# A row maximum over 64 MB: blocks of 2, 14, 96 and 16 rows per partition in place of 112 and 16

## The chip, the core and the metric

The kernel runs on one core of a Trainium2 chip. Its engines are PE (the matrix engine, whose weight loads are listed as PEld), DVE (the vector engine), ACT (the scalar engine), POOL (the general engine) and SP, which here only issues transfers. Sixteen DMA engines move data between HBM and the on-chip memory, which has 128 partitions. The metric is the time of one execution on the device in microseconds (us). The profile is of one such execution.

## The reference

```python
def setup_inputs():
    batch, seq, dim = 32, 512, 1024
    return {"x": np.random.randn(batch, seq, dim).astype(np.float32)}

def reference(x):
    return np.max(x, axis=-1).astype(np.float32)
```

The input is 16384 rows of 1024 float32 values, 64 MB; the output is the largest value of each row, 64 KB.

## The kernel before

**Blocks.** The 16384 rows are 128 rows for each of the 128 partitions. `BLOCKS` (L13) says how they are dealt out. A block of S rows per partition is a stretch of 128 x S rows that lies in one piece in HBM; partition p holds rows p x S to p x S + S - 1 of it. Before the change there are two blocks, of 112 and of 16 rows per partition (the second list sums to 14, and `last`, 2, comes to it for the tail). Within a block each number of the list is one load: so many rows of every partition, that is 128 runs, one in each partition, each in one piece in HBM. The runs of one load lie S rows (S x 4 KB) apart: 448 KB in the first block, 64 KB in the second. Loads are numbered through all blocks, 0 to 17. Load 0 has 2 rows, load 1 has 15, load 2 has 16.

**The ring.** All loads land in one tile, `ring`, with places for `RING = 47` rows per partition, and go around it: a load that doesn't fit in what is left starts again at place 0. `issue` (the inner function that calls `nc.sync.dma_start`, L238) issues loads in order on SP, each as early in the program as the reductions that read its places have been written down. A load into places that an earlier load had waits on SP until that load's reduction is done, and the loads behind it in SP's queue wait with it. Each load uses one of eight semaphores in turn, and waits too until the load that used it eight loads earlier has landed.

**The order of the work.** `PLAN` (L31) is an order written out by hand. `d3` reduces load 3 on DVE: one instruction for all its rows, written by `maximum` (L78). `t` and `b` steps send parts of some late rows the other way: PE transposes them (L160), ACT copies the result (L166), POOL takes the maximum across partitions (L168), and PE turns the answer back (L178). `p` steps reduce the rest of those rows on DVE, `m` steps merge, and `f0` to `f3` reduce the four pieces into which the last two rows of each partition are cut (loaded at L243). `in_turn` keeps each engine to the order of the plan.

**The stores.** The results lie in the first 128 columns of the ring's tile (`res`), one column for each row of a partition. `views` has one entry for each block: where its results go in HBM, and their columns. All but the last are stored (L265) behind `behind`, which is the reduction `f0`; the last block's store (L267) comes after the last reduction. Both are issued from ACT, after its copies.

What the change touches: `BLOCKS`, and through it the HBM address of every load ahead of load 11, the sizes of loads 1 and 4, the places of loads 2 to 10 in the ring with the reductions that they wait for, and the number of entries in `views`.

Of the kernel before, what the change touches and what calls it, by code (L numbers as in the profile page):

```python
# [10 lines left out]


BLOCKS = [  # L13
    [2, 15, 16, 14, 11, 11, 10, 10, 8, 8, 7],
    [3, 3, 3, 2, 1, 1, 1],
]
RING = 47
# [279 lines left out]
```

## Time and profile before

| | |
|---|---|
| Median of 3 runs | 163.83 us (163.79 to 163.84) |
| Profiled execution, from first to last instruction (span) | 162.1 us |
| DVE busy | 135.3 us (83% of the span), 33 instructions |
| PE, PEld, ACT, POOL busy | 13.6, 11.7, 6.3 and 15.9 us |
| Read from HBM, written | 67.11 MB, 0.07 MB |
| Mean rate over the span | 414 GB/s |

The span is counted within the profiled execution; the median is of whole executions, which hold something more around it. "Idle before" is the time in which an engine had nothing running just before an instruction, and the name behind it is what ended that time. A queue's share is the time that its packets took, out of the time of all 16 DMA engines. A line of the chain of waits that names DMA covers the time from a transfer's issue to its landing, so time spent queued behind other transfers is in it. L numbers are lines of the kernel as printed above.

The reductions, one instruction for each of the loads: 10 rows take 10.82 us (mean of two), 11 rows 11.88, 16 rows 17.22. SP's queue waited 90.8 us in all for reductions (7 times) and 31.2 us for landings of loads (3 times) before it issued at L238. The two stores landed 1.6 and 1.4 us after their issue.

### The profile page before, as it was taken

How to read it: one execution, taken by the hardware profiler on the slowest of the kernel's cores; microseconds unless marked ns; L12 is line 12 of the kernel's file. 1: busy time of each engine (PE TensorE's matmuls, PEld its weight loads, DVE VectorE, ACT ScalarE, POOL GpSimd, SP SyncE). 2: the span in 40 equal slices, each digit the busy share in tenths (PEclk: the TensorE clock that was granted, in tenths of full speed). 3: DMA queues.
4: the chain of work that ended last, by engine and by line, in shares of the span. 5: the costliest groups of instructions: out<-in, count | busy, mean ns of one | idle time of the engine just before them, and what ended most of it. 6: DMA issues, size and time to landing. Idle time of an engine off the chain costs nothing.

```text
span 162.1 us, 295 instructions
## 1 busy us (share of the span) xinstructions
PE 13.6 (8%) x76; PEld 11.7 (7%) x76; DVE 135.3 (83%) x33; ACT 6.3 (4%) x7; POOL 15.9 (10%) x10
## 2 busy tenths in 40 slices
PE   0000000000000000000000000000000000772942
PEld 0000000000000000000000000000000000762731
DVE  3500019998399999999999999996999999999994
ACT  3000000000000000000000000000000000241120
POOL 0000000000000000000000000000000000099791
PEclk9999999999999999999999999999999999996555
DMA  5995999599879999898999799799999989999991
GB/s 178 566 485 258 470 501 517 259 517 517 354 340 439 453 404 534 356 523 367 478 411 475 334 485 475 334 485 388 477 429 388 466 382 446 415 421 416 411 388 34
DMA packets 3456, 67.18 MB, mean 414 GB/s; under 512 B 640, under 2 KB 896, under 8 KB 1536
## 3 DMA queue, kind: packets, MB, share of 16 engines
q1 hardware_dynamic: 3168, 67.11, 96.8%
q10 hardware_dynamic: 288, 0.07, 0.2%
HBM read 67.11 MB, written 0.07 MB: 414 GB/s over the span
## 4 chain that ended last, share of the span: by engine, by line
DMA 50%; DVE 47%; SPq 1%; issue 0%; DVEq 0%
DMA ring<-in_x_dram 50%; DVE ring L78 45%; DVE joint L78 2%; SPq L238 1%; DVEq L292 0%
## 5 line engine op out<-in xcount | busy, mean ns | idle before, releaser
L78 DVE TENSOR_REDUCE ring<-ring 128x1 f32<-128x1024 f32 (+13 forms) x20 | 129.9, 6547 | 23.5 <-DMA ring<-in_x_dram 23.5
L168 POOL PARTITION_ALL_REDUCE top<-sb x6 | 15.7, 2658 | 142.6 <-ACT sb L166 142.5
L160 PE MATMUL ps<-ident,ring 128*128 128x128 f32 x38 | 9.0, 423 | 140.0 <-DMA ring<-in_x_dram 140.0
L160 PEld LDWEIGHTS ps<-ident,ring 128*128 128x128 f32 x38 | 7.6, 225 | 140.1 <-issue 140.1
L166 ACT COPY sb<-ps 128x1024 f32<-128x1024 f32 (+2 forms) x6 | 5.0, 834 | 150.5 <-PE ps L160 143.5
L78 DVE TENSOR_REDUCE joint<-ring 128x2 f32<-128x1280 f32 (+1 forms) x3 | 3.9, 1314 | 0.0
L178 PE MATMUL got<-ident,top 1*128 1x1 f32 x24 | 2.7, 228 | 3.8 <-POOL top L168 3.6
L178 PEld LDWEIGHTS got<-ident,top 1*128 1x128 f32 x24 | 2.4, 188 | 4.6 <-POOL top L168 4.6
L178 PE MATMUL joint<-ident,top 1*128 1x1 f32 x14 | 2.0, 244 | 1.9 <-POOL top L168 1.9
L178 PEld LDWEIGHTS joint<-ident,top 1*128 1x128 f32 x14 | 1.7, 210 | 2.7 <-POOL top L168 2.7
L166 ACT ACT_TABLE_LOAD x1 | 1.3, 1283 | 0.7 <-PEq L281 0.7
L83 DVE MEMSET ident<- 128x128 f32 x1 | 0.2, 165 | 0.8 <-PEq L281 0.8
L90 DVE TENSOR_SCALAR rowno<-rowno 32x1 f32<-32x1 f32 x3 | 0.4, 146 | 0.1
L85 DVE TENSOR_TENSOR_SCAN colno<-ident 128x128 f32<-128x128 f32 x1 | 0.4, 425 | 0.0
L92 DVE TENSOR_SCALAR ident<-colno,rowno 128x128 f32<-128x128 f32 x1 | 0.3, 288 | 0.0
L87 DVE STREAM_TRANSPOSE rowno<-colno 128x32 f32<-128x32 f32 x1 | 0.2, 211 | 0.0
L78 DVE TENSOR_REDUCE ring<-got 128x3 f32<-128x24 f32 x1 | 0.2, 172 | 0.0
L78 DVE TENSOR_REDUCE ring<-joint 128x5 f32<-128x20 f32 x1 | 0.2, 170 | 0.0
L281 POOL MEMSET const-float32-0.0<- 128x1 f32 x1 | 0.1, 98 | 0.2 <-issue 0.2
L281 POOL MEMSET const-bfloat16-1.0<- 128x1 bf16 x1 | 0.1, 102 | 0.0
L281 POOL MEMSET const-uint8-127<- 128x1 uint8 x1 | 0.1, 101 | 0.0
L281 POOL MEMSET const-float32-1.0<- 128x1 f32 x1 | 0.1, 98 | 0.0
(1 smaller groups left out, 0.1 us busy)
## 6 DMA issues: line engine op xcount, KB each, us to landing
ring<-in_x_dram SPq DMA_DIRECT2D x2, 5632.0 KB, 29.9
ring<-in_x_dram SPq DMA_DIRECT2D x2, 5120.0 KB, 36.8
ring<-in_x_dram SPq DMA_DIRECT2D x2, 4096.0 KB, 32.5
ring<-in_x_dram SPq DMA_DIRECT2D x1, 7680.0 KB, 22.6
ring<-in_x_dram SPq DMA_DIRECT2D x1, 7168.0 KB, 58.0
ring<-in_x_dram SPq DMA_DIRECT2D x3, 1536.0 KB, 35.7
ring<-in_x_dram SPq DMA_DIRECT2D x1, 3584.0 KB, 29.2
ring<-in_x_dram SPq DMA_DIRECT2D x2, 1024.0 KB, 17.8
```

Of the source, the lines that this page charges most:

```text
L78: return in_turn("DVE", nc.vector.reduce_max(out=out, in_=in_, axis=X))
L83: in_turn("DVE", nc.vector.memset(ident, 1.0))
L85: in_turn("DVE", nc.vector.tensor_tensor_scan(out=colno, data0=ident, data1=ident, initial=-1.0, op0=ALU.add, op1=ALU.mult))
L87: in_turn("DVE", nc.vector.transpose(out=rowno, in_=colno[:, :32]))
L90: in_turn("DVE", nc.vector.tensor_scalar(out=part, in0=part, scalar1=float(q * 32), scalar2=None, op0=ALU.add))
L92: identity = in_turn("DVE", nc.vector.tensor_scalar(out=ident, in0=colno, scalar1=rowno[:, 0:1], scalar2=None, op0=ALU.is_equal))
L160: in_turn("PE", nc.tensor.transpose(out=ps[:, w:w + P], in_=rows(j)[:, lead[j] + r + i, c * P:(c + 1) * P], identity=ident,))
L166: in_turn("ACT", nc.scalar.copy(out=sb[:, :W], in_=ps[:, :W]))
L168: in_turn("POOL", nc.gpsimd.partition_all_reduce(top[:, :W], sb[:, :W], P, bass_isa.ReduceOp.max))
L178: in_turn("PE", nc.tensor.transpose(out=share(j)[:, r + i, c:c + 1], in_=tops[k][0:1, w:w + P], identity=ident[0:1, 0:1],))
L238: load = nc.sync.dma_start(out=rows(issued), in_=src)
L281: nc = _bacc.Bacc("TRN2", target_bir_lowering=False, num_devices=1)
```

## The change

One list is replaced. The first block's 112 rows per partition become three blocks of 2, 14 and 96.

```diff
 BLOCKS = [
-    [2, 15, 16, 14, 11, 11, 10, 10, 8, 8, 7],
+    [2],
+    [14],
+    [16, 14, 12, 11, 10, 10, 8, 8, 7],
     [3, 3, 3, 2, 1, 1, 1],
 ]
 RING = 47
```

Load 0 is now a whole block of 2 rows per partition, so that its 128 runs of 8 KB lie one behind the other in HBM: one megabyte in one piece. Load 1 is a whole block of 14 rows per partition, seven megabytes in one piece. Loads 2 to 10 read a block of 96 rows per partition, in which the runs of one load lie 384 KB apart. Loads 11 to 17 and the pieces of the tail are as before. Load 1 has 14 rows and not 15, load 4 has 12 and not 11; the number of loads, their order and the plan stay.

There are four entries in `views` and so four stores: three on ACT behind `f0`, of 2, 14 and 96 columns (8, 56 and 384 bytes in each partition), and the last, of 16 columns, as before. The second and third of them wait on semaphores that loads 15 and 16 used.

With 14 rows in load 1, loads 0 to 3 take 46 places, and the loads that go around the ring after them lie elsewhere: load 4 in places 0 to 12 (before: 0 to 11), load 5 in 12 to 23 (11 to 22), load 6 in 23 to 33 (22 to 32), load 7 in 33 to 43 (32 to 42), and loads 8, 9, 10 and on where they were. Load 6 now waits for the reduction of load 3, where before it was load 2's, and load 10 for that of load 5, where before it was load 6's.

## The prediction

> **What bounds the kernel now.** I read the chain of waits first, then the timeline of DVE, the page's DMA queues, and the DMA view cut into short windows. The chain (start, duration, what):
>
> ```profile
> 1.62 41.49 DMA ring<-in_x_dram
> 43.11 0.02 issue
> 43.13 66.55 DVE ring L78 x5
> ...
> 111.01 38.94 DMA ring<-in_x_dram
> ```
>
> Read alone it says DMA, then DVE, then DMA. The timeline of DVE (start, busy time, group, idle time before it and what ended that) shows who really hands over:
>
> ```profile
> 5.65 2.29 DVE L78 TENSOR_REDUCE ring<-ring 128x2 f32<-128x2048 f32 x1 [3.14 <-DMA ring<-in_x_dram]
> 23.78 16.15 DVE L78 TENSOR_REDUCE ring<-ring 128x15 f32<-128x15360 f32 x1 [15.85 <-DMA ring<-in_x_dram]
> 43.13 66.53 DVE L78 TENSOR_REDUCE ring<-ring 128x16 f32<-128x16384 f32 x5 [3.20 <-DMA ring<-in_x_dram]
> 110.97 40.23 DVE L78 TENSOR_REDUCE ring<-ring 128x10 f32<-128x10240 f32 x7 [1.30 <-DMA ring<-in_x_dram]
> ```
>
> DVE waits for a load four times, the last time for load 7 at 110.97. From there it runs with gaps of at most 0.09 us until its last reduction ends at 159.83, 48.9 us. So the end is "landing of load 7, plus 48.9 us of DVE work". Load 7 lands when the load queue has moved the 89 rows per partition of loads 0 to 7, and that queue is never idle (page; packets, MB, share of 16 engines):
>
> ```profile
> q1 hardware_dynamic: 3168, 67.11, 96.8%
> q10 hardware_dynamic: 288, 0.07, 0.2%
> ```
>
> 0.968 x 162.1 = 156.9 us of transfer: all the time from 1.7 us, when the first packets start, to about 158.6. Hence the end moves with the speed of the load stream, and a DVE operation before load 7 can move by up to 1.30 us for nothing.
>
> **The rows moved from load 1 to load 4.** Load 1 goes from 15 rows to 14, load 4 from 11 to 12. Line by form (op, shapes, count, busy us, mean ns):
>
> ```profile
> L78 DVE TENSOR_REDUCE ring<-ring 128x15 f32<-128x15360 f32 x1 | 16.2, 16154 | 15.8 <-DMA ring<-in_x_dram 15.8
> ...
> L78 DVE TENSOR_REDUCE ring<-ring 128x14 f32<-128x14336 f32 x1 | 15.1, 15076 | 0.0
> ```
>
> One row is 16.154 - 15.076 = 1.08 us on DVE. In the stream it is 128 x 4 KB = 0.524 MB, and from 60 to 75 us the stream moved 433 GB/s: 1.21 us. Loads 1, 2 and 3 land 1.21 us earlier; loads 4 onward land when they did, since 58 rows lie up to load 4 in both. DVE: d2 starts at 43.13 - 1.21 = 41.92; the five operations d2 to d6 take 66.53 + 1.08 = 67.61 and end at 109.53 instead of 109.66. DVE then waits 1.4 us for load 7 instead of 1.30. Effect on the end: 0. If the 1.30 us of cover were gone, that 0.13 us would be all it is worth.
>
> **The ring moves.** Loads 0 to 3 now fill 46 of 47 places. Load 4 takes places 0 to 12, load 5 12 to 23, load 6 23 to 33, load 7 33 to 43, load 8 0 to 8, load 9 8 to 16, load 10 16 to 23; from load 11 on places are the old ones. So load 6 now overlaps load 3 and must wait for d3, not d2. On SP it moves from 60.4 to d3's end, about 74.1, and is issued beside load 7, which waited for d3 already: nothing is queued between them that goes later. At 74.1 the stream still has load 5 to move: load 2 (33 rows) was in by 43.13, load 5 ends 36 rows later, 43.13 + 36 x 1.21 = 86.7 us. With 1.0 us from an issue to its first packet (0.72 to 1.7 at the start) the cover is 11 us; below zero, each us would be a us at the end. Load 10 goes the other way, from d6 (109.69) to d5 (98.7); loads 11 to 13, behind it on SP, still wait for d6 and go out at 109.6, with loads 8 and 9 and now 10 ahead of them. Cost 0.
>
> **Two more stores on ACT.** One store of 112 columns becomes three of 2, 14 and 96. All three stand behind the first reduction of the tail pieces and ahead of the last store:
>
> ```profile
> 158.01 0.38 ACTq L265 DMA_DIRECT2D out_dram<-ring  x1
> ...
> 159.66 0.17 DVE L78 TENSOR_REDUCE ring<-joint 128x5 f32<-128x20 f32 x1
> 159.86 0.34 ACTq L267 DMA_DIRECT2D out_dram<-ring  x1
> ```
>
> ACT sits idle from 158.39 to 159.86, waiting for the last reduction. Three issues of 0.38 with 0.05 us between (the gap between SP's issues in the chain) end at 158.01 + 1.24 = 159.25: 0.6 us spare. With SP's dearest issue, 0.61 us, they end at 159.94, and the last store is 0.08 us late. Their packets: q10's 288 took 0.002 x 16 x 162.1 = 5.2 engine-us, 18 ns each. Two stores more are 288 more packets, 0.32 us on each engine, between 159.2 and the last store's packets at 160.7; the loads are over at 158.6. The semaphore waits of the added stores are for loads 15 and 16, whose reductions are over by 156.4. At the end SP has two more completions to look at, at 0.05 us an issue gap 0.1 us. I take 0, the ends are 0 and +0.2.
>
> The Trainium skill (DMA: Bandwidth & Descriptors, Specifications) says that a transfer under 512 B turns into a read-modify-write, which speaks against cutting 448 B runs into 8, 56 and 384 B. Both old stores, 448 B and 64 B, are under that figure already and the row has 18 ns for each packet; by the rule, even at twice that price, the packets would still end before the last store's start.
>
> **The addresses.** Load 0 stays 128 runs of 8 KB, load 1 128 runs of 56 KB; only where the runs begin changes: a pitch of 448 KB becomes 8 KB, 56 KB, and 384 KB for the 96-row block. No row shows those pitches, but the last block is read at 64 KB. The DMA view for a window with 8 KB packets at pitch 448 KB (load 0, 3.2 to 4.4 us) and one with 8 KB packets at pitch 64 KB (load 14, 149.6 to 151.2 us):
>
> ```profile
> q1 hardware_dynamic: 63, 0.52, 101.7%
> ```
>
> ```profile
> q1 hardware_dynamic: 83, 0.68, 101.7%
> ```
>
> 1.017 x 16 x 1.2 / 63 = 0.310 us a packet, and 1.017 x 16 x 1.6 / 83 = 0.314. A seven times smaller pitch, a power of two, moves the price by 1.2%, and windows this short count their edges roughly. I take 0 for the new pitches; the ends are -1.2% and +1.2% of the 109 us up to load 7, -1.3 to +1.3 us. The lower end I trust less: a packet's price is the same all through the big loads, as for an engine at its own limit, so a kinder address should have nothing to give.
>
> The Trainium skill (the same page, Latency and other measured facts) lists 207 GB/s at a row pitch of 512 KiB against 214 with the pitch padded, and advises contiguous tiles or padding: a rule that favours the first two blocks and leaves the third, 3 x 128 KiB, open. By its 3.4% on the whole 96-row block the sum would be some 4 us higher, about 168; 448 and 64 KiB, the pitches of this trace, show nothing of the kind.
>
> The start is the other unknown. The window from 1.6 to 2.6 us, with the rate by its 40 slices (a packet counts where it starts):
>
> ```profile
> GB/s 0 0 0 0 0 983 328 328 0 0 655 328 0 0 0 0 0 328 0 328 328 0 328 328 0 0 0 0 0 0 328 0 328 0 0 0 328 0 0 0
> ...
> q1 hardware_dynamic: 16, 0.13, 77.0%
> ```
>
> 0.770 x 16 x 1.0 / 16 = 0.77 us a packet, 0.46 more than at 3.2 us: the first packets start cold. If scattered addresses cause that, one contiguous megabyte saves up to 0.46 us; if sixteen neighbours get in each other's way, it may cost as much again. I take 0: the sixteen starts are spread over 0.8 of that microsecond, load 0 lands with the engine that starts last, and a late start is set by the issue, which the change leaves as it is.
>
> **Sum.** Span 162.1 + 0 (rows) + 0 (ring) + 0 (stores) + 0 (addresses) = 162.1. Around it lie 163.83 - 162.1 = 1.7 us in the runs shown, which nothing here touches: 163.8.
>
> **Rivals.** (1) The cold start goes away: 163.83 - 0.46 = 163.4. For it, the 0.77 us against 0.31; against it, the engine that starts last. (2) DVE's earlier start reaches the end: 163.83 - 1.21 = 162.6. Against it stands the 1.30 us wait at 110.97, which swallows it. (3) Slower: the 384 KB pitch makes the stream from load 2 on dearer. Each per cent is 0.69 us (the 69 us from 42 to 111), all of it at the end, since DVE waits for load 7 already; it decides from 0.5%, and at 1.2% gives 163.83 + 0.83 = 164.7. For it, the 0.314 against 0.310; against it, the even price of packets at 448 KB. (4) The stores come late by 0.2 to 0.5 us, on ACT or behind 8 B packets: 164.2. Against it, the 0.6 us spare.
>
> **How the numbers follow.** About 0.2% (0.33 us) is what a measurement of this kernel can tell from no change. Forecast, nothing moves by that much: 0.53. Rival 1: 0.15, rival 2: 0.04, together faster 0.19. Rival 3: 0.19, rival 4: 0.09, together slower 0.28. The forecast's own range is 163.5 to 164.15. For 8 in 10 the range goes down to rival 1 and up to most of rival 3: 163.35 to 164.7.
>
> **What would show it.** Right: DVE again waits about 1.4 us for load 7 and starts on it at 111.0 within 0.2; load queue at 96 to 97%; the first packets again near 0.77 us; three store issues done before 159.5 and the last at 159.9. A load 7 landing near 110.5 means rival 1, near 112 rival 3; an ACT issue of the last store long after the last reduction means rival 4. The forecast is wrong most simply if packets of the 96-row block take longer than their size did before.

## The result and the profile after

| | before | changed |
|---|---|---|
| Median | 163.84 us (163.79 to 163.93) | 165.96 us (165.75 to 166.33) |
| Ratio, 95% interval | | 1.013 (1.0118 to 1.0141) |
| Span of the profiled execution | 162.1 us | 163.9 us |

The change costs 2.1 us. The views of the profile show where they are. (The profiled execution of the changed kernel took 165.75 us, the fastest of its runs; its span is 163.95 us with two decimals.) First DVE's timeline, from the first reduction of 16 rows on:

```profile
41.86 67.74 DVE L80 TENSOR_REDUCE ring<-ring 128x16 f32<-128x16384 f32 x5 [4.27 <-DMA ring<-in_x_dram]
110.91 40.23 DVE L80 TENSOR_REDUCE ring<-ring 128x10 f32<-128x10240 f32 x7 [1.30 <-DMA ring<-in_x_dram]
```

Load 2 is there 1.27 us earlier than before (1.21 was forecast), and load 7 starts to be reduced at 110.91, which was 110.97. So nothing was lost in the loads, the ring or the reductions. The timeline of ACT and DVE at the end agrees (start, duration, line):

```profile
157.95 1.34 ACTq L267 DMA_DIRECT2D out_dram<-ring  x3
...
159.61 0.17 DVE L80 TENSOR_REDUCE ring<-joint 128x5 f32<-128x20 f32 x1
159.81 0.34 ACTq L269 DMA_DIRECT2D out_dram<-ring  x1
```

The three stores are issued by 159.29, and the last one leaves at 159.81, 0.05 us earlier than before. The whole loss lies behind that: from the last store's issue to the end of the span it was 162.1 - 159.86 = 2.2 us, and now is 163.95 - 159.81 = 4.1. The page's issues of the stores, in KB and median us from issue to landing, before the change and after it:

```profile
out_dram<-ring ACTq DMA_DIRECT2D x1, 56.0 KB, 1.6
...
out_dram<-ring ACTq DMA_DIRECT2D x1, 8.0 KB, 1.4
```

```profile
out_dram<-ring ACTq DMA_DIRECT2D x1, 48.0 KB, 4.0
...
out_dram<-ring ACTq DMA_DIRECT2D x1, 1.0 KB, 3.0
out_dram<-ring ACTq DMA_DIRECT2D x1, 7.0 KB, 2.7
out_dram<-ring ACTq DMA_DIRECT2D x1, 8.0 KB, 3.2
```

The 8 KB store at the end is the same store in both, and lands 3.2 us after its issue where it took 1.4. SP waits for the landings at the end. Its waits for stores (us in total, times, longest) come to 2.2 us before the change and 4.5 after it:

```profile
SPq L292 <- DMA out_dram<-ring: 2.2, 2, 1.6
```

```profile
SPq L294 <- DMA out_dram<-ring: 4.5, 1, 4.5
```

Yet the packets take no longer. DMA's busy share from 157 to 164 us in 40 slices of 0.175 us, and the queue of the stores in that window (packets, MB, share of 16 engines), before the change and after it:

```profile
DMA  9999998300082000000004000000000000000000
...
q10 hardware_dynamic: 288, 0.07, 4.3%
```

```profile
DMA  9999998300210400730004000000000000000000
...
q10 hardware_dynamic: 576, 0.07, 6.5%
```

0.043 x 16 x 7 us / 288 is 17 ns a packet before the change, and 0.065 x 16 x 7 us / 576 is 13 ns after it. After the loads come four groups in the changed kernel, one for each store; the last is over by 160.9. The packets have gone out, and for two microseconds nothing is busy; only the landings fail to come (the last at 159.81 + 3.2 = 163.0). A packet's time, then, doesn't say when a store has landed.

### The profile page after: what moved, and what is told of

Same layout as the page of the kernel before. It is cut to its first block, busy times and chain, and to the rows that moved or that the text cites. A ratio compares the mean times of both kernels' runs of the same rounds, so it can differ in the third digit from the quotient of the medians.

```text
span 163.9 us, 296 instructions
## 1 busy us (share of the span) xinstructions
PE 12.8 (8%) x76; PEld 11.0 (7%) x76; DVE 135.4 (83%) x33; ACT 6.3 (4%) x7; POOL 15.9 (10%) x10
## 4 chain that ended last, share of the span: by engine, by line
DMA 64%; DVE 32%; SPq 1%; issue 0%; DVEq 0%
DMA ring<-in_x_dram 64%; DVE ring L80 30%; DVE joint L80 2%; SPq L240 1%; DVEq L294 0%
## 5 line engine op out<-in xcount | busy, mean ns | idle before, releaser
L162 PE MATMUL ps<-ident,ring 128*128 128x128 f32 x38 | 7.9, 382 | 139.9 <-DMA ring<-in_x_dram 139.4
L162 PEld LDWEIGHTS ps<-ident,ring 128*128 128x128 f32 x38 | 6.6, 202 | 140.0 <-issue 140.0
```

What stands on the lines that cost most here:

```text
L162: in_turn("PE", nc.tensor.transpose(out=ps[:, w:w + P], in_=rows(j)[:, lead[j] + r + i, c * P:(c + 1) * P], identity=ident,))
```

## The experiments

Every kernel was timed beside the kernel before on the same chip. The first four ask whether it is the number of the stores, the size of their runs, or how the runs lie.

**Blocks of 16, 96 and 16.** The edit is against the changed kernel. Loads 0 and 1 still read eight megabytes in one piece, but as one block, so that the runs of each of the two lie 64 KB apart; the stores have runs of 64, 384 and 64 bytes.

```diff
-    [2],
-    [14],
+    [2, 14],
```

> Blocks of 16 (loads of 2 and 14), 96 and 16 rows: three stores of 64, 384 and 64 bytes in each partition. Theory A (a store whose runs are not whole 64-byte pieces lands late, and those behind it with it): no such run is left, 163.8 us, last landing 1.4 us after its issue. Theory B (each store more at the end costs about 1 us, whatever its size): one store more than before, about 164.9. Theory C (many runs in one 64-byte piece of HBM get in each other's way): none shared, 163.8. If it is the 384-byte store itself that lands late: 165 or more.

Measured: 164.2 us against 163.7, ratio 1.0026 (1.0014 to 1.0038). All three stores land as before:

```profile
out_dram<-ring ACTq DMA_DIRECT2D x1, 48.0 KB, 1.6
out_dram<-ring ACTq DMA_DIRECT2D x2, 8.0 KB, 1.4
```

The 48 KB store, 4.0 us in the changed kernel, is the same store here. It is not slow itself. Theory B is too dear: the loss is 0.43 us by the ratio, and no landing shows it. The trace of this run has a loss of that size in the loads: load 2 is first read at 41.64 and load 7 at 111.04, 69.40 us apart, where the changed kernel, with the same addresses for these loads, has 110.91 - 41.86 = 69.05. Why they took longer stays open.

**The old loads, the first store cut evenly in three.** The edit is against the kernel before.

```diff
-    for dst, src in views[:-1]:
-        store = nc.scalar.dma_start(out=dst, in_=src)
+    for c0, c1 in ((0, 32), (32, 64), (64, 112)):
+        dst, src = views[0]
+        dst = bass.AP(tensor=dst.tensor, offset=dst.offset + c0, ap=[[112, P], [1, c1 - c0]])
+        store = nc.scalar.dma_start(out=dst, in_=src[:, c0:c1])
```

> The kernel before with its first store cut into three of 32, 32 and 48 columns (128, 128 and 192 bytes): four stores, whole 64-byte pieces. Theory A: 163.8. Theory B: as the changed kernel, 165.9. Theory C: 163.8. If every run under 512 bytes costs alike, 384 runs in place of 128: between 165 and 167.

Measured: 163.88 against 163.7, ratio 1.0008 (0.9998 to 1.0017). Four stores with 384 runs under 512 bytes in place of 128, and the last still lands in 1.4 us. The number of stores is out as the cause, and so is a price for every short run.

**The same cut at columns 2, 14 and 96.** The edit is that of the run before with `((0, 2), (2, 16), (16, 112))`.

> The kernel before, loads untouched, with its first store cut into columns 2, 14 and 96 (8, 56 and 384 bytes, the runs of one store 448 bytes apart). Theory A: the 8 and 56 byte runs are no whole 64-byte pieces, as slow as the changed kernel, 165.5 to 166.2. Theory B: 165.9. Theory C: a 64-byte piece is shared by two runs only, one of each store, in place of eight: 163.8 to 164.5.

Measured: 163.86 against 163.7, ratio 1.001 (1.0 to 1.0019):

```profile
out_dram<-ring ACTq DMA_DIRECT2D x1, 1.0 KB, 1.4
out_dram<-ring ACTq DMA_DIRECT2D x1, 7.0 KB, 1.5
out_dram<-ring ACTq DMA_DIRECT2D x1, 8.0 KB, 1.4
```

These are the sizes of the changed kernel to the byte, and nothing is late. Theory A falls: 8 and 56 byte runs are not slow as such. What differs is where they lie, 448 bytes apart here, end to end there.

**The changed kernel with its two small stores early.** The lines left out are marked by dots.

```diff
             readers[k] -= 1
+            if step == "d1":
+                for dst, src in views[:2]:
+                    nc.scalar.dma_start(out=dst, in_=src)
...
-    for dst, src in views[:-1]:
+    for dst, src in views[2:-1]:
```

> The changed kernel with the stores of 2 and 14 columns issued as soon as load 1 is reduced, some 38 us in, and only those of 96 and 16 at the end. Theories A and C: the two late landings are over long before the end, 163.8, last landing 1.4 us after its issue. Theory B: as before, two stores at the end, 163.8. If the 384-byte store itself lands late: 165 or more. It also shows what the new loads alone are worth: 163.8 by the trace, in which load 7 is reduced from 110.91.

Measured: 164.98 against 163.7, ratio 1.0095 (1.006 to 1.0129), a miss for every theory, but a telling one. The stores at the end are quick again (1.5 and 1.4 us), and the loss has gone to the middle:

```profile
7.91 30.19 ACTq L256 DMA_DIRECT2D out_dram<-ring  x2
22.62 15.09 DVE L80 TENSOR_REDUCE ring<-ring 128x14 f32<-128x14336 f32 x1 [14.74 <-DMA ring<-in_x_dram]
42.79 32.21 DVE L80 TENSOR_REDUCE ring<-ring 128x16 f32<-128x16384 f32 x2 [5.08 <-DMA ring<-in_x_dram]
```

The first of the two, 8 bytes a run, waits for load 0 alone and goes out at 7.91. Load 1 is late by 0.11 us against the changed kernel, load 2 by 0.93 (42.79 against 41.86), and this stays to the end: load 7 is first read at 111.82. The load queue in the window from 24.3 to 27 us (packets, MB, share; a packet counts whole where it starts, so the share can pass 100%), here and in the changed kernel:

```profile
q1 hardware_dynamic: 16, 1.05, 110.5%
q10 hardware_dynamic: 16, 0.00, 0.3%
```

```profile
q1 hardware_dynamic: 28, 1.84, 156.7%
```

1.105 x 16 x 2.7 / 16 = 2.98 us for a packet of 64 KB while 8 byte packets go between them, and 1.567 x 16 x 2.7 / 28 = 2.42 without them. The 8 byte packets themselves take next to nothing; the 16 load packets beside them take 0.56 us more. But 8 byte packets are not enough to slow a load. From 16 to 21 us, too, this run has one of them for each load packet (32 and 32), and the load queue reads, here and in the changed kernel:

```profile
q1 hardware_dynamic: 32, 1.84, 85.0%
```

```profile
q1 hardware_dynamic: 32, 1.84, 84.7%
```

0.850 x 16 x 5 / 32 = 2.13 us and 0.847 x 16 x 5 / 32 = 2.12 us for a packet of 56 KB: hardly a difference. So early issue takes the loss off the end of the kernel, and the loads come some 0.9 us later; most of it lies in one group of load packets, and why in that one was not tried.

**Which store, and whether the loads matter at all.** In the next runs the list `STORES` stands for names each store outright: first column, number of columns, where its first run begins in the output, and the distance of its runs, the last two counted in values of 4 bytes. The kernel that the stores are put into is the one before, but for the second of the four. "The run before" in what was expected of the third run is the first of the four.

```diff
-    for dst, src in views[:-1]:
-        store = nc.scalar.dma_start(out=dst, in_=src)
+    for c0, n, at0, step in STORES:
+        dst = bass.AP(tensor=of.tensor, offset=of.offset + at0, ap=[[step, P], [1, n]])
+        store = nc.scalar.dma_start(out=dst, in_=res[:, c0:c0 + n])
```

Old loads, the changed kernel's stores: `((0, 2, 0, 2), (2, 14, 256, 14), (16, 96, 2048, 96))`.

> The loads of the kernel before, the stores of the changed one: columns of 2, 14 and 96 packed in HBM so that the runs of one store lie end to end (8, 56 and 384 bytes apart). The rows of the output are permuted: column c of partition p goes where the changed kernel would put it. If the stores alone make the change slow (theory C): 165.5 to 166.3, the last landing 3 us after its issue. If the loads have a part in it: under 165.

Measured: 166.11 against 163.68, ratio 1.0148 (1.0133 to 1.0163), and the last store lands 3.4 us after its issue. The stores alone make the whole loss.

New loads, the old stores: `((0, 112, 0, 112),)` in the changed kernel.

> The loads of the changed kernel with the two stores of the kernel before (112 columns, 448 bytes apart, and 16). The rows of the output are permuted. If the loads are worth nothing, as the prediction had it: within 0.2% of the kernel before, 163.4 to 164.0. If the pitch of 384 KB costs something: above 164.0. If the contiguous start gains: below 163.4.

Measured: 163.9 against 163.68, ratio 1.0012 (1.0003 to 1.0022). The last store lands in 1.4 us. By the interval the new loads cost 0.05 to 0.36 us; the ratio itself, 0.12%, is within the 0.2% forecast.

8 byte runs 64 bytes apart, 56 byte runs end to end: `((0, 2, 0, 16), (2, 14, 2048, 14), (16, 80, 3840, 80))`.

> As the run before, but the 8 byte runs lie 64 bytes apart, each in a 64-byte piece of its own; the 56 byte runs stay end to end; the third store has 80 columns (320 bytes). Parts of the output stay unwritten. Theory C1 (eight 8-byte runs in one 64-byte piece are what is slow): 163.9. Theory C2 (the 56 byte runs, most of which cross from one piece to the next): 165 or more.

Measured: 163.91 against 163.68, ratio 1.0012 (1.0003 to 1.0021).

8 byte runs end to end, 56 byte runs 64 bytes apart: `((0, 2, 0, 2), (2, 14, 256, 16), (16, 80, 2304, 80))`.

> The other way round: the 8 byte runs end to end, the 56 byte runs 64 bytes apart, each in a piece of its own, 80 columns in the third store. Parts of the output stay unwritten. Theory C1: 165 to 166. Theory C2: 163.9. If both share the loss, this and the run before lie between.

Measured: 166.33 against 163.68, ratio 1.0164 (1.0146 to 1.0183). The stores of the first of these two and of the second, KB and us to landing:

```profile
out_dram<-ring ACTq DMA_DIRECT2D x1, 40.0 KB, 1.6
...
out_dram<-ring ACTq DMA_DIRECT2D x1, 1.0 KB, 1.5
out_dram<-ring ACTq DMA_DIRECT2D x1, 7.0 KB, 1.8
out_dram<-ring ACTq DMA_DIRECT2D x1, 8.0 KB, 1.4
```

```profile
out_dram<-ring ACTq DMA_DIRECT2D x1, 40.0 KB, 4.5
...
out_dram<-ring ACTq DMA_DIRECT2D x1, 1.0 KB, 3.4
out_dram<-ring ACTq DMA_DIRECT2D x1, 7.0 KB, 3.4
out_dram<-ring ACTq DMA_DIRECT2D x1, 8.0 KB, 3.9
```

C1 holds and C2 falls. The one kilobyte with its 128 runs of 8 bytes end to end is slow, and the stores issued after it are late behind it, whatever their own runs.

**How close is too close?** Old loads, `((0, 2, 0, 8), (2, 14, 1024, 16), (16, 80, 3072, 80))`: 8 byte runs 32 bytes apart.

> The loads of the kernel before, the first store's columns 2, 14 and 80; the 8 byte runs lie 32 bytes apart (two in each 64-byte piece), the 56 byte runs 64 apart. Parts of the output stay unwritten. If the loss goes by how many runs share a 64-byte piece, a quarter of it or less is left: 163.9 to 164.4. If any sharing costs the whole: 166. If a piece of 32 bytes is what counts: 163.9.

Measured: 163.95 against 163.8, ratio 1.0008 (0.9999 to 1.0018).

`((0, 2, 0, 4), (2, 14, 512, 16), (16, 80, 2560, 80))`: 16 bytes apart.

> As the run before with the 8 byte runs 16 bytes apart (four in each 64-byte piece, two in each 32). Parts of the output stay unwritten. If the loss goes by the runs in a 64-byte piece: between that run and the 166.3 us of the packed runs, 164.5 to 165.5. If any sharing costs the whole: 166. If only runs that touch each other are slow: 163.9.

Measured: 164.91 against 163.8, ratio 1.0064 (1.0043 to 1.0086).

`((0, 4, 0, 4), (4, 12, 512, 16), (16, 80, 2560, 80))`: 16 byte runs end to end.

> Columns of 4, 12 and 80: runs of 16 bytes end to end (four in each 64-byte piece), 48 byte runs 64 bytes apart. Parts of the output stay unwritten. If the loss goes by the number of runs in a 64-byte piece: as the run before, whatever that gives. If it goes by the size of a run: less than 166, since each is twice as long. If touching is what counts: 165 or more while the run before is at 163.9.

Measured: 164.78 against 163.8, ratio 1.006 (1.0045 to 1.0075). The last store, 8 KB, in the last two runs:

```profile
out_dram<-ring ACTq DMA_DIRECT2D x1, 8.0 KB, 2.4
```

```profile
out_dram<-ring ACTq DMA_DIRECT2D x1, 8.0 KB, 2.5
```

| first store: run, distance of run starts | ratio | last store lands after |
|---|---|---|
| 8 bytes, 448 | 1.0010 | 1.4 us |
| 8 bytes, 64 | 1.0012 | 1.4 us |
| 8 bytes, 32 | 1.0008 | 1.4 us |
| 8 bytes, 16 | 1.0064 | 2.4 us |
| 16 bytes, 16 | 1.0060 | 2.5 us |
| 8 bytes, 8 | 1.0164 | 3.9 us |
| 8 bytes, 8 (the changed kernel's stores, old loads) | 1.0148 | 3.4 us |

The loss goes with the distance between the starts of the runs, not with their size (8 or 16 bytes at the same distance) nor with their touching (8 bytes at 16 have gaps). The forecasts by the number of runs in a piece of 64 bytes came true in all three runs, and "any sharing costs the whole" fell; pieces of 32 bytes, which no two runs share at 32 and two share at 16, fit as well. The time follows the last landing: 3.9 - 1.4 = 2.5 us, and 1.64% of 163.68 is 2.7.

## Why the prediction was wrong

**The bound, the rows and the ring: right.** d2 was put at 41.92 and came at 41.86; load 7 was to be reduced from 111.0 within 0.2 and was from 110.91, behind a wait of 1.30 where 1.4 was forecast. The load queue's work is 0.957 x 163.95 = 156.9 us, as before. Load 6, held until d3, didn't keep the queue waiting. One small thing was overlooked: load 6 lies 10 rows, 10 x 1.21 = 12.1 us, ahead of load 7 in the stream, and DVE, now earlier, ran into its landing. In the chain of the changed kernel it is issued at 74.10 and lands 24.66 us later, at 98.76; d6 starts at 98.78. So d2 to d6 took 67.74 us and not 67.61, and the 0.1 us came out of the wait for load 7.

**The addresses: right.** The new loads with the old stores cost 0.12%. Rival 3, the 384 KB pitch, put 0.8 us there. The Trainium skill's list of rates by row pitch (DMA: Bandwidth & Descriptors, Latency and other measured facts), measured on copies between HBM tensors and taken at its 3.4%, would by estimate have asked for some 4 us; loads at a pitch of 3 x 128 KiB show no such loss here.

**The cold start: right in effect.** The first packets took 0.697 x 16 x 1.0 / 18 = 0.62 us each in the window from 1.6 to 2.6 us, where it was 0.77, and load 0 was first read at 5.61 instead of 5.65. Most of the excess over 0.31 is there for contiguous addresses too. Of rival 1's 0.46 us 0.04 came, and even these are not shown to be a gain: with the old loads the traces here have load 0 first read anywhere from 5.29 to 5.65.

**The early start swallowed: right.** Rival 2's 1.21 us ended in the wait for load 7.

**"Two more stores on ACT": the step that failed.** Its counts nearly held: the issues were over at 159.29 (159.25 forecast; the three took 1.34 us and not 1.24, from a start 0.06 us earlier), and the packets of the added stores were over before the last store's. Then it took "0, the ends are 0 and +0.2", because it priced a store by its issue and its packets. The landing, 1.6 and 1.4 us for the runs of 448 and 64 bytes before, got no term, and without a reason was taken to stay as it was for runs of 8. That landing was the term to bound, and no row of the trace before had runs so close together. What the runs showed in its place: behind 128 runs of 8 bytes end to end, the last store of the changed kernel, itself as before, lands after 3.2 us, 1.8 later; nothing hides it at the end, and the span grows by 163.95 - 162.1 = 1.85 (the median by 2.1). Rival 4 named the stores, with 0.2 to 0.5 us, but for ACT's queue or the packets' time; neither came later, and what was held against it, the 0.6 us to spare on ACT (0.5 was left), lies ahead of the loss and could not hide it. The rule of the Trainium skill on transfers under 512 B (the same page, Specifications) was weighed and put aside by twice a packet's price. The runs of 8 bytes 32 to 448 bytes apart, and those of 56, 64 and 384 bytes where no closely packed runs went ahead, all lie under its figure and land in 1.4 to 1.8 us; the rule points the right way, but it can't tell the slow store from the quick ones, and no run here shows whether a read-modify-write is what holds the landings up.

## What to carry to other kernels

A store's cost has a third term beside issue and packets: the landing. Where nothing follows the last store it lies open on the end of the kernel: of the 2.2 us from the last store's issue to the end of the span before, 1.4 were its landing. When a layout is recut, look at the stores too, and at how far apart in HBM the runs of neighbouring partitions start: here, for 128 runs in one store, 32 bytes or more cost next to nothing, 16 cost 1 us, and 8 cost 2.1 to 2.7. Moving such a store earlier need not make it free: in the one run that did, the loads came 0.9 us later.

## What the runs showed of the hardware

Many short runs close together in HBM hold up the landing of the stores issued after them, though the packets of all of them look short: behind 128 runs of 8 bytes end to end a store of 40 KB landed 4.5 us after its issue instead of 1.6, and the last store up to 3.9 instead of 1.4. The step lies between 32 and 16 bytes from start to start. Whether what counts is the number of runs in one piece of 64 (or 32) bytes, or the smallness of the area that all 128 fall into (1 KB at 8, 2 KB at 16, 4 KB at 32), was not tried apart: in every store here the two go together. Nor was it tried whether runs of one piece written by different DMA engines do the same, and where the time goes between the last packet and the landing no view here tells.

For loads in flight beside such a store there is one run: a group of load packets of 64 KB took 2.98 us instead of 2.42, others beside the same 8 byte packets took no longer.

No version here beats the kernel before; of the other ways to cut the rows into blocks only 16, 96 and 16 was tried, and it gives back most of the loss, at 1.0026.
